# Moving the later adaLN sums of a hybrid decoder layer in VectorE's order, with weights loaded two pieces ahead

## The chip, the core and the metric

One core of a Trainium2 chip runs the kernel. Its engines are called as the profile calls them: PE (TensorE, matrix products; PEld is its loading of weights), DVE (VectorE), ACT (ScalarE), POOL (GpSimd) and SP (SyncE, which issues most transfers). The metric is the device time of one execution in microseconds (us), the median over runs.

## What is computed

One decoder layer on 256 tokens of width 2048, in float32, with matrix products accurate to about float32 (each operand is split into a rounded high part and a low rest). Cut to what matters here:

```python
c_act = silu(c)                                    # one vector of 2048
mod = c_act @ w_mod + b_mod                        # w_mod is 2048 x 12288
shift1, scale1, gate1, shift2, scale2, gate2 = split(mod, 6)     # vectors 0 to 5
u = rms(h, norm1_w) * (1 + scale1) + shift1
proj = u @ w_in                                    # q, k, v of two mixers, z, gates
o_a = stick_breaking(qa, ka, va)                   # 16 heads
o_b = gated_delta_rule(qb, kb, vb, g, beta)        # 16 heads, after a causal convolution
merged = sigmoid(gate_a) * (o_a @ p_a) + sigmoid(gate_b) * (o_b @ p_b)
h = h + gate1 * (merged @ w_out)
u = rms(h, norm2_w) * (1 + scale2) + shift2
h = h + gate2 * ((silu(u @ w_gate) * (u @ w_up)) @ w_down)
```

There are six adaLN vectors of 2048 columns; numbers 0 and 1 are needed at once, 2 (`gate1`) for the output projection, 3 and 4 (`shift2`, `scale2`) for the feed-forward part, 5 (`gate2`) at its end.

## The kernel before

**Jobs and steps.** All large products run through `run_jobs`. A job is one 512-column block of a weight, a step is 256 rows of it (512 KB). For a step, SP loads `raw` (four buffers; the load of step n+4 is issued behind the low split of step n, L277 to L300), ACT rounds it to `wh` (L284), DVE subtracts to get `wl` (a line of `tt`, L119), three steps ahead of use, and PE multiplies activations with both (`mm`, L116; written `acc`). There are two calls of `run_jobs`: the first has the q, k, v blocks of both mixers, three z blocks and the first gate; the second has `p_a`, the last z block, the second gate, `p_b`, `w_out` and the whole feed-forward part.

**Work beside the products.** After each quarter of a step, `beat` advances two queues of Python generators: `convs` (the convolution, on DVE) and `chains`: first four delta-rule chains (`gdn_chain`, one per group of four heads, tiles named `gw`), then four attention chains (`sb_chain`, tiles `sbw`, `SPh`). A delta-rule chain is a long line of small DVE steps between two 128x512 stream transposes, and then of small products (`pb_X`, `pb_Q`, ...) on PE. PE's queue is in order: a `pb_X` whose operand is late holds up every `acc` product behind it.

**The later adaLN sums** are the `background` queue. Every `bg_every` ticks (a tick is half a step) `pump_bg` advances one generator by one yield. `mod_steps` (L176) loads one piece of `w_mod`, 128 rows by 1024 columns, 512 KB, called `wm`, through SP, one piece ahead in two buffers, and adds it, multiplied by one element of `c` per partition, to the sums `macc` (128 x 2048) on DVE (through `stt`, L122; 1024 columns at a time). A vector takes 32 pieces. The 128 partitions are then added up: for vectors 3 and 4 by transposes on PE and accumulating copies on ACT (`mod_cols`, L201), for the gate vectors 2 and 5 by a product with ones (`mod_bcast`, L213). In the first call (`bg_every=3`, from tick 200 on) vectors 3 and 4 are queued, in the second (`bg_every=6`) vector 2, and from the start of the feed-forward part vector 5; in the wide gate jobs of that part a pump comes every 2 ticks, in its up jobs none.

**What sets the order.** The Python program only writes the work down. The framework's planner then lists each engine's instructions by its own estimate of when operands are there, so an instruction can stand far ahead of where it was written. `tc.keep_in_program_order(ins)` ties one instruction behind the instruction written before it on the same engine.

Of the kernel before, what the change touches and what calls it, by code (L numbers as in the profile page):

```python
# [9 lines left out]
F32 = mybir.dt.float32  # L10
F32R = mybir.dt.float32r
AF = mybir.ActivationFunctionType
ALU = mybir.AluOpType
# [3 lines left out]
P = 128  # L17
D = 2048
T = 256
NB = T // P  # L20
KT = D // P
# [6 lines left out]
MW = 1024  # L28
# [4 lines left out]
PUMP_GA = 1.3  # L33
NZ = 3
BGF = 200
BGE = 3
H2 = 5
RG = 2
SMA = 8
# [56 lines left out]
def body(tc, cst, x, c, w_mod, b_mod, norm1_w, w_in, q_norm_w, k_norm_w, conv_w, a_log, dt_bias,  # L96
         o_norm_w, p_a, p_b, w_out, norm2_w, w_gate, w_up, w_down, out, dbg=None):
    nc = tc.nc
    ctx = ExitStack()
    x, w_mod, b_mod, w_in, p_a, p_b, w_out, w_gate, w_up, w_down, out, conv_w = (  # L100
        t[0] for t in (x, w_mod, b_mod, w_in, p_a, p_b, w_out, w_gate, w_up, w_down, out, conv_w))
# [7 lines left out]
    def bank(name, tag="ms"):  # L109
        return ps.tile([P, 512], F32, tag=tag, name=name)  # L110
# [26 lines left out]
    def tr(o, i):  # L137
        nc.tensor.transpose(o, i, ident)
# [19 lines left out]
    n1c, n2c, cc = cols[:, 0:16], cols[:, 16:32], cols[:, 32:48]  # L158
    onc = cols[:, 50:51]
    bsh1, bsc1, bsh2, bsc2 = (cols[:, 64 + 16 * i:80 + 16 * i] for i in range(4))  # L160
# [10 lines left out]
        nc.gpsimd.tensor_tensor(out=o, in0=i, in1=half[:, 0:o.shape[-1]], op=ALU.pow)  # L171


    def mod_steps(i, acc, pool, width, bufs, row, cc=cc):
        v0 = i * D
        if row:  # L176
            nc.gpsimd.memset(acc, 0.0)
            nc.sync.dma_start(out=acc[0:1], in_=b_mod[v0:v0 + D].rearrange("(o d) -> o d", o=1))
        parts = [(k, j) for k in range(KT) for j in range(0, D, width)]
        tiles = {}  # L180

        def load(n):
            k, j = parts[n]
# [15 lines left out]
    def mod_cols(acc, o, bias):  # L199
        for j in range(4):  # L200
            b = bank("pb_mod")  # L201
            for i in range(4):
                tr(b[:, i * P:(i + 1) * P], acc[:, (4 * j + i) * P:(4 * j + i + 1) * P])
            for i in range(4):
                k = 4 * j + i

                act(b[:, i * P:(i + 1) * P], b[:, i * P:(i + 1) * P], AF.Copy, accum_out=o[:, k:k + 1])
            yield
        tt(o, o, bias, ALU.add)
        yield  # L210

    def mod_bcast(acc, o, pool):
        for j in range(4):  # L213
            sl = slice(j * 512, (j + 1) * 512)
            hi = pool.tile([P, 512], F32R, tag="c2", name="bch", bufs=4)
            lo = pool.tile([P, 512], F32R, tag="c2", name="bcl", bufs=4)
            nc.scalar.copy(out=hi, in_=acc[:, sl])
            tt(lo, acc[:, sl], f32(hi), ALU.subtract)
# [5 lines left out]
            yield  # L224


    chains = deque()
# [9 lines left out]
    tph = {}  # L237
# [18 lines left out]
            pump(1000)  # L256

    background = deque()

    def pump_bg(n=1):  # L260
# [109 lines left out]
    mcols = cp.tile([P, 4, KT], F32, name="mcols")  # L370
# [567 lines left out]
    jobs = []  # L938
# [161 lines left out]
    def mod_col_task(i, slot):  # L1100
        acc = tph["tp"].tile([P, D], F32, tag="macc", name="macc", bufs=1)
        yield from mod_steps(i, acc, tph["tp"], MW, 2, False)
        yield from mod_cols(acc, mcols[:, slot], {3: bsh2, 4: bsc2}[i])

    background.append(mod_col_task(3, 3))
    background.append(mod_col_task(4, 2))
    st = {}


    def z_done(n):  # L1110
# [109 lines left out]


    def gate_task(i, key, cc):
        acc = tq.tile([P, D], F32, tag="macc2", name="macc2", bufs=1)
        yield from mod_steps(i, acc, tq, 1024, 2, True, cc)
        st[key] = tq.tile([P, D], F32, tag="gbc", name=key, bufs=1)
        yield from mod_bcast(acc, st[key], tq)
# [22 lines left out]


    def ffn_begin():
        r2 = cp.tile([P, 2], F32, name="r2")
        for b in range(NB):
            act(ss[:, 3, 4 * b:4 * b + 4], ss[:, 2, 4 * b:4 * b + 4], AF.Identity, scale=1.0 / D, bias=eps4, accum_out=r2[:, b:b + 1])
        rstd2 = cp.tile([P, 2], F32, name="rstd2")
        rsqrt(rstd2, r2)
        b2 = cp.tile([P, KT], F32, tag="gate", name="b2", bufs=1)
        nc.gpsimd.tensor_copy(out=b2, in_=mcols[:, 3])
        nc.vector.tensor_scalar(out=mcols[:, 2], in0=mcols[:, 2], scalar1=1.0, scalar2=None, op0=ALU.add)
        tt(mcols[:, 2], mcols[:, 2], n2c, ALU.mult)  # L1260
# [132 lines left out]
```

## Time and profile before

| | before |
|---|---|
| runs, us | 2080.69, 2071.72, 2079.27 (median 2079.27) |
| profiled execution, us | 2075.31, its span 2073.4 |
| PE busy | 1987.6 us (96%) |
| DVE busy | 1380.0 us (67%) |
| ACT busy | 1061.7 us (51%) |
| transfers | 449.72 MB, mean 217 GB/s |
| chain that ended last, by engine | PE 83%, DMA 7%, DVE 5% |

The span is the time from the first to the last instruction; the execution's own time has 1.9 us around it. Busy times are averages over stages with different limits, so what counts is read stage by stage: where PE, the busiest engine, stands still, and what it waited for there. A row of a wait says who waited, on which line, for whom, how long in total and how often. A granted clock (PEclk) of 1.00 is 2.4 GHz; the only other level is 1.2 GHz, so 0.91 over 20 us is a part of that stretch at half speed.

### The profile page before, as it was taken

How to read it: one execution, taken by the hardware profiler on the slowest of the kernel's cores; microseconds unless marked ns; L12 is line 12 of the kernel's file. 1: busy time of each engine (PE TensorE's matmuls, PEld its weight loads, DVE VectorE, ACT ScalarE, POOL GpSimd, SP SyncE). 2: the span in 40 equal slices, each digit the busy share in tenths (PEclk: the TensorE clock that was granted, in tenths of full speed). 3: DMA queues.
4: the chain of work that ended last, by engine and by line, in shares of the span. 5: the costliest groups of instructions: out<-in, count | busy, mean ns of one | idle time of the engine just before them, and what ended most of it. 6: DMA issues, size and time to landing. Idle time of an engine off the chain costs nothing.

```text
span 2073.4 us, 29277 instructions
## 1 busy us (share of the span) xinstructions
PE 1987.6 (96%) x11097; PEld 1719.3 (83%) x11097; DVE 1380.0 (67%) x1846; ACT 1061.7 (51%) x1766; POOL 114.0 (5%) x139
## 2 busy tenths in 40 slices
PE   1999999999999999999999999999999999999998
PEld 1899999987888788887888888788888888888887
DVE  4987989987557876667654555787656555555554
ACT  3346676675666568443454444554455334445432
POOL 4311010110100000000000000000000000000000
PEclk9899999999999999999999999999999999999999
DMA  8996663665557874888766566598755556655563
GB/s 302 386 329 201 194 193 119 208 193 164 167 177 246 291 242 144 255 303 297 237 187 195 184 220 194 178 304 301 227 180 188 195 191 188 190 185 186 190 211 134
DMA packets 208551, 449.72 MB, mean 217 GB/s; under 512 B 16101, under 2 KB 16536, under 8 KB 207896
## 3 DMA queue, kind: packets, MB, share of 16 engines
q1 hardware_dynamic: 198906, 413.25, 62.1%
q0 software_dynamic: 9504, 34.61, 4.5%
q8 instruction: 87, 1.43, 0.3%
q14 instruction: 54, 0.44, 0.1%
HBM read 445.70 MB, written 2.10 MB: 216 GB/s over the span
## 4 chain that ended last, share of the span: by engine, by line
PE 83%; DMA 7%; DVE 5%; issue 2%; ACT 2%; POOL 0%; SPq 0%; DVEq 0%; ACTq 0%; POOLq 0%
PE acc L116 76%; DMA wm<-in_w_mod 4%; DVE wl L119 2%; DMA smod<-in_w_mod 1%; DMA crow<-in_conv_w 1%; PE pb_mod L116 1%; PE pb_Q L116 1%; DVE macc L122 1%; DMA raw<-in_w_in 0%; PE pb_oa L116 0%; PE pb_z L116 0%; ACT wh L284 0%; PE pb_X L116 0%; PE pb_af L116 0%; DVE gw L119 0%
## 5 line engine op out<-in xcount | busy, mean ns | idle before, releaser
L119 DVE TENSOR_TENSOR wl<-raw,wh 128x1024 fp32r<-128x1024 f32 x648 | 789.0, 1221 | 482.2 <-ACT wh L284 479.6
L284 ACT CAST wh<-raw 128x1024 fp32r<-128x1024 f32 x648 | 680.2, 1051 | 768.0 <-PE acc L116 626.4
L116 PE MATMUL acc<-u,wh 128*128 128x512 f32 x1408 | 495.8, 397 | 0.0
L116 PE MATMUL acc<-u,wl 128*128 128x256 f32 x1408 | 395.6, 281 | 2.1 <-DVE wl L119 2.1
L116 PEld LDWEIGHTS acc<-u,wh 128*128 128x128 f32 x1408 | 264.3, 188 | 63.8
L116 PE MATMUL acc<-wh,uh 128*128 128x512 f32 x768 | 307.2, 400 | 0.0
L116 PE MATMUL acc<-wl,uh 128*128 128x512 f32 x768 | 300.6, 391 | 0.0
L116 PE MATMUL acc<-wh,ul 128*128 128x512 f32 x768 | 300.2, 391 | 0.0
L116 PEld LDWEIGHTS acc<-u,wl 128*128 128x128 f32 x1408 | 266.0, 189 | 3.6 <-DVE wl L119 3.3
L116 PE MATMUL acc<-uh,wh 128*128 128x256 f32 x768 | 221.2, 291 | 1.7 <-ACT part L935 1.7
L116 PE MATMUL acc<-uh,wl 128*128 128x256 f32 x768 | 219.4, 287 | 0.0
L116 PE MATMUL acc<-ul,wh 128*128 128x256 f32 x768 | 218.7, 286 | 0.0
L116 PE MATMUL acc<-wh,ff 128*128 128x512 f32 x704 | 216.9, 389 | 0.0
L116 PEld LDWEIGHTS acc<-wl,uh 128*128 128x128 f32 x768 | 144.5, 188 | 30.5
L116 PEld LDWEIGHTS acc<-wh,ul 128*128 128x128 f32 x768 | 144.8, 189 | 27.3
L116 PEld LDWEIGHTS acc<-wh,uh 128*128 128x128 f32 x768 | 144.9, 189 | 26.9
L122 DVE SCALAR_TENSOR_TENSOR macc<-wm,cols,macc 128x1024 f32<-128x1024 f32 x92 | 117.7, 1282 | 59.7 <-DMA wm<-in_w_mod 59.4
L116 PEld LDWEIGHTS acc<-wh,ff 128*128 128x128 f32 x704 | 132.0, 188 | 27.4
L116 PEld LDWEIGHTS acc<-uh,wh 128*128 128x128 f32 x768 | 149.1, 196 | 2.7 <-ACT part L935 1.9
L116 PEld LDWEIGHTS acc<-ul,wh 128*128 128x128 f32 x768 | 148.9, 194 | 0.4
L116 PEld LDWEIGHTS acc<-uh,wl 128*128 128x128 f32 x768 | 148.3, 194 | 0.4
L116 PE MATMUL acc<-wl,ff 128*128 128x512 f32 x352 | 137.0, 389 | 0.0
(289 smaller groups left out, 2268.9 us busy)
## 6 DMA issues: line engine op xcount, KB each, us to landing
raw<-in_w_in SPq DMA_DIRECT2D x286, 512.0 KB, 4.3
wm<-in_w_mod SPq DMA_DIRECT2D x128, 512.0 KB, 5.2
raw<-in_w_gate SPq DMA_DIRECT2D x88, 512.0 KB, 4.3
raw<-in_w_up SPq DMA_DIRECT2D x88, 512.0 KB, 4.4
raw<-in_w_down SPq DMA_DIRECT2D x88, 512.0 KB, 4.2
smod<-in_w_mod POOLq DMA_DIRECT2D x64, 512.0 KB, 11.2
raw<-in_p_a SPq DMA_DIRECT2D x32, 512.0 KB, 5.5
raw<-in_p_b SPq DMA_DIRECT2D x32, 512.0 KB, 3.6
```

The lines of the kernel that those rows point to most:

```text
L116: nc.tensor.matmul(o, lhsT=lhsT, rhs=rhs, start=start, stop=stop, skip_group_check=True)
L119: nc.vector.tensor_tensor(out=o, in0=a, in1=b, op=op)
L122: nc.vector.scalar_tensor_tensor(out=o, in0=a, scalar=s, in1=b, op0=op0, op1=op1, **kw)
L284: nc.scalar.copy(out=wh, in_=raws[n])
```

## The change

Four things are changed together.

1. **Order on DVE.** Every sum of a later adaLN vector is tied behind the DVE instruction written before it (`keep_in_program_order`). It can no longer be listed ahead of its place.
2. **Halves.** A vector is summed in two halves of 1024 columns, all 16 pieces of one half first, in one `macc` of 128 x 1024; the final addition over partitions follows each half (512 columns per yield).
3. **Loads two pieces ahead**, in three buffers (`MRB = 3`), one load to a pump before the first sum.
4. **Where the vectors stand.** Only vector 3 stays in the first call, with a pump every 6 ticks; vectors 2 and 4 are in the second call, with a pump every 3 ticks (`BGD`), and 5 in the feed-forward part as before. `wo_begin` pumps only until vector 2 is done, and `ffn_begin` pumps out the rest.

```diff
-BGE = 3
+BGE = 6
+BGD = 3
+MRB = 3
...
-    def mod_steps(i, acc, pool, width, bufs, row, cc=cc):
+    def mod_parts(i, pool, row, cc, use):
         v0 = i * D
-        parts = [(k, j) for k in range(KT) for j in range(0, D, width)]
+        parts = [(h, k) for h in range(D // MW) for k in range(KT)]
         tiles = {}
...
-            t = pool.tile([P, width], F32, tag="mraw", name=f"wm{i}_{n}", bufs=bufs)
-            nc.sync.dma_start(out=t, in_=w_mod[k * P:(k + 1) * P, v0 + j:v0 + j + width])
+            t = pool.tile([P, MW], F32, tag="mraw", name=f"wm{i}", bufs=MRB)
+            nc.sync.dma_start(out=t, in_=w_mod[k * P:(k + 1) * P, v0 + h * MW:v0 + (h + 1) * MW])
             tiles[n] = t
 
-        load(0)
-        for n, (k, j) in enumerate(parts):
-            if n + 1 < len(parts):
-                load(n + 1)
+        for n in range(MRB - 1):
+            load(n)
+            yield
+        for n, (h, k) in enumerate(parts):
+            if n + MRB - 1 < len(parts):
+                load(n + MRB - 1)
+            if k == 0:
+                acc = pool.tile([P, MW], F32, tag="macc", name="macc", bufs=1)
+                if row:
+                    nc.gpsimd.memset(acc, 0.0)
+                    nc.sync.dma_start(out=acc[0:1], in_=b_mod[v0 + h * MW:v0 + (h + 1) * MW].rearrange("(o d) -> o d", o=1))
+                    yield
             t = tiles.pop(n)
             if k or row:
-                stt(acc[:, j:j + width], t, cc[:, k:k + 1], acc[:, j:j + width], ALU.mult, ALU.add)
+                ins = nc.vector.scalar_tensor_tensor(out=acc, in0=t, scalar=cc[:, k:k + 1], in1=acc, op0=ALU.mult, op1=ALU.add)
             else:
-                nc.vector.tensor_scalar(out=acc[:, j:j + width], in0=t, scalar1=cc[:, 0:1], scalar2=None, op0=ALU.mult)
+                ins = nc.vector.tensor_scalar(out=acc, in0=t, scalar1=cc[:, 0:1], scalar2=None, op0=ALU.mult)
+            tc.keep_in_program_order(ins)
             yield
+            if k == KT - 1:
+                for j in range(MW // 512):
+                    yield from use(h * (MW // 512) + j, acc[:, j * 512:(j + 1) * 512])
...
-    background.append(mod_col_task(3, 3))
-    background.append(mod_col_task(4, 2))
+    background.append(mod_cols(3, mcols[:, 3], bsh2, BgPool(), cc))
...
     background.append(gate_task(2, "g1", cc))
+    background.append(mod_cols(4, mcols[:, 2], bsc2, tq, cc))
...
-        pump_bg(1000)
+        while "g1" not in ready:
+            pump_bg(1)
...
     def ffn_begin():
+        pump_bg(1000)
...
-    run_jobs(jobs, bg_every=6)
+    run_jobs(jobs, bg_every=BGD)
```

**The order it makes.** Three places in the listed order matter below. `macc` is a sum, `wl` a low split, `gw` the third delta-rule chain's tiles, `gq` and `gk` the convolution.

DVE, in the third delta-rule chain, between its two 128x512 stream transposes. Before:

```order
L119 TENSOR_TENSOR gw_3902<-gw_3901 128x112
L122 SCALAR_TENSOR_TENSOR macc<-wm_17_5883,cols,macc 128x1024
L119 TENSOR_TENSOR gw_3901<-gw_3901,gw_3902 128x14x8
L119 TENSOR_TENSOR wl<-raw,wh 128x1024
L119 TENSOR_TENSOR gw_3902<-gw_3901 128x112
L122 SCALAR_TENSOR_TENSOR macc<-wm_18_5929,cols,macc 128x1024
L119 TENSOR_TENSOR gw_3901<-gw_3901,gw_3902 128x16x7
```

After:

```order
L121 TENSOR_TENSOR gw_3901<-gw_3901,gw_3902 128x12x9
L121 TENSOR_TENSOR gw_3902<-gw_3901 128x112
L121 TENSOR_TENSOR gw_3901<-gw_3901,gw_3902 128x14x8
L121 TENSOR_TENSOR gw_3902<-gw_3901 128x112
L121 TENSOR_TENSOR gw_3901<-gw_3901,gw_3902 128x16x7
L121 TENSOR_TENSOR wl<-raw,wh 128x1024
```

The sums have gone from between the chain's steps, and so have some of the splits and convolution steps: from the first stream transpose to the last of the 16 small ones, 9 `wl`, 3 sums and 16 convolution steps stood there before; now there are 6, none and 5. In all, 32 sums stood ahead of the 114th `wl` before; now the first stands behind the 112th `wl`, followed by one about every three `wl` up to the 210th; those of vectors 2 and 4 lie between the 257th and the 371st `wl`, and those of vector 5 between the 391st and the 459th.

PE, at the first small product of the same chain; `acc_4466` and `acc_4467` are the two accumulators of one 512-column block, `wh_4334` the first weight tile of that block. Before:

```order
L116 MATMUL acc_4467<-uh_212,wh_4562 128x256
L116 MATMUL acc_4467<-ul_213,wh_4562 128x256
L116 MATMUL acc_4467<-uh_212,wl_4564 128x256
L116 MATMUL pb_X_4345<-gw1_3902 64x64 x4
L116 MATMUL acc_4467<-uh_212,wh_4562 128x256
```

After:

```order
L118 MATMUL acc_4466<-uh_212,wl_4336 128x256
L118 MATMUL acc_4467<-uh_212,wh_4334 128x256
L118 MATMUL pb_X_4345<-gw1_3902 64x64 x4
L118 MATMUL acc_4467<-ul_213,wh_4334 128x256
L118 MATMUL acc_4467<-uh_212,wl_4336 128x256
```

The chain's first small product now stands 98 `acc` products of 256 columns earlier. In the first and second chain it stands 35 and 9 such products earlier, in the fourth 47 products of 512 columns.

DVE, at the start of the heads of the third attention chain (`sbw<-pb_z` is the first thing DVE does for a head, `SPl` what PE waits for). Before:

```order
L122 SCALAR_TENSOR_TENSOR macc<-wm_16_7406,cols,macc 128x1024
L122 SCALAR_TENSOR_TENSOR macc<-wm_17_7444,cols,macc 128x1024
L119 TENSOR_TENSOR wl<-raw,wh 128x1024 x2
L122 SCALAR_TENSOR_TENSOR macc<-wm_18_7480,cols,macc 128x1024
L119 TENSOR_TENSOR wl<-raw,wh 128x1024
L122 SCALAR_TENSOR_TENSOR macc<-wm_19_7530,cols,macc 128x1024
L119 TENSOR_TENSOR wl<-raw,wh 128x1024
L122 SCALAR_TENSOR_TENSOR macc<-wm_20_7570,cols,macc 128x1024
L122 SCALAR_TENSOR_TENSOR sbw<-pb_z,a 128x384 x2
L119 TENSOR_TENSOR sbw<-sbw,cs 128x2x128
L119 TENSOR_TENSOR wl<-raw,wh 128x1024
L119 TENSOR_TENSOR SPl<-sbw,SPh 128x384
```

After:

```order
L202 SCALAR_TENSOR_TENSOR macc<-wm_6872,cols,macc 128x1024
L202 SCALAR_TENSOR_TENSOR macc<-wm_6947,cols,macc 128x1024
L121 TENSOR_TENSOR wl<-raw,wh 128x1024 x6
L202 SCALAR_TENSOR_TENSOR macc<-wm_7010,cols,macc 128x1024
L124 SCALAR_TENSOR_TENSOR sbw<-pb_z,a 128x384 x2
L121 TENSOR_TENSOR sbw<-sbw,cs 128x2x128
L121 TENSOR_TENSOR wl<-raw,wh 128x1024
L121 TENSOR_TENSOR SPl<-sbw,SPh 128x384
```

Five sums stood within four splits there; now one stands behind six splits.

## Rows read from the trace of the kernel before

**Rows 1.** Busy time by stage: us, engines' busy (instructions), PEclk, DMA share, GB/s.

```profile
170.00:330.00 160.00, 155.13 (x1307) 151.91 (x1306) 143.75 (x315) 108.97 (x250) 14.81 (x15) 0.99 0.61 189
330.00:450.00 120.00, 113.66 (x970) 108.39 (x969) 107.58 (x234) 79.89 (x220) 16.62 (x19) 0.97 0.55 172
450.00:510.00 60.00, 56.15 (x338) 45.68 (x337) 52.30 (x121) 43.01 (x94) 4.90 (x4) 1.00 0.64 192
510.00:640.00 130.00, 129.92 (x632) 108.78 (x631) 73.16 (x100) 85.92 (x211) 9.69 (x9) 1.00 0.53 160
...
700.00:730.00 30.00, 25.44 (x110) 20.73 (x109) 23.88 (x28) 14.44 (x23) 0.00 (x0) 0.94 0.86 291
...
850.00:930.00 80.00, 80.00 (x354) 66.26 (x353) 53.20 (x44) 34.90 (x36) 0.00 (x0) 1.00 0.88 296
930.00:990.00 60.00, 55.84 (x238) 43.80 (x236) 42.98 (x38) 22.04 (x23) 0.00 (x0) 1.00 0.88 299
...
1050.00:1276.00 226.00, 226.00 (x1016) 186.66 (x1015) 122.43 (x120) 102.10 (x115) 1.81 (x1) 1.00 0.61 197
1335.00:1435.00 100.00, 100.00 (x576) 87.84 (x575) 79.26 (x83) 47.21 (x61) 0.00 (x0) 1.00 0.89 300
1435.00:1460.00 25.00, 22.86 (x128) 19.31 (x127) 20.18 (x21) 10.25 (x15) 0.00 (x0) 1.00 0.89 312
```

**Rows 2.** Groups in 850:930: busy us, mean ns, idle before them and its end.

```profile
L116 PE MATMUL acc<-wh,uh 128*128 128x512 f32 x118 | 45.9, 389 | 0.0
L119 DVE TENSOR_TENSOR wl<-raw,wh 128x1024 fp32r<-128x1024 f32 x27 | 32.5, 1220 | 7.8 <-ACT wh L284 7.6
L122 DVE SCALAR_TENSOR_TENSOR macc<-wm,cols,macc 128x1024 f32<-128x1024 f32 x17 | 21.8, 1285 | 17.7 <-DMA wm<-in_w_mod 17.4
```

**Rows 3.** Groups in 930:990.

```profile
L116 PE MATMUL acc<-wh,oah 128*128 128x512 f32 x77 | 30.1, 390 | 0.0
L122 DVE SCALAR_TENSOR_TENSOR macc<-wm,cols,macc 128x1024 f32<-128x1024 f32 x14 | 18.0, 1284 | 18.7 <-DMA wm<-in_w_mod 18.7
```

**Rows 4.** Instructions on `wm`, whole span: time from issue to landing.

```profile
DMA to landing us min/median/max: 3.4/5.2/6.8
```

**Rows 5.** Timeline of DVE, 696:717: start, us, instruction, [idle before, its end].

```profile
708.62 1.28 DVE L122 SCALAR_TENSOR_TENSOR macc<-wm,cols,macc 128x1024 f32<-128x1024 f32 x1 [4.43 <-DMA wm<-in_w_mod]
```

**Rows 6.** Timeline of PE, 709:716.

```profile
714.10 0.45 PE L116 MATMUL pb_af<-SPh,rmask 128*128 128x384 f32 x1 [3.95 <-ACT SPh L1039]
715.16 0.69 PE L116 MATMUL pb_af<-SPl,rmask 128*128 128x384 f32 x1 [0.61 <-DVE SPl L119]
```

**Rows 7.** Busy time by stage, shorter stretches, columns as in rows 1.

```profile
78.00:104.00 26.00, 23.79 (x164) 23.08 (x165) 22.41 (x27) 8.36 (x12) 9.57 (x14) 0.80 1.03 386
...
710.00:730.00 20.00, 15.44 (x65) 12.64 (x65) 19.01 (x24) 9.66 (x15) 0.00 (x0) 0.91 0.88 294
```

**Rows 8.** Timeline of PE at the chains' first small products, four windows.

```profile
250.13 0.45 PE L116 MATMUL pb_X<-gw 128*64 128x64 f32 x8 [2.44 <-issue]
...
335.13 0.45 PE L116 MATMUL pb_X<-gw 128*64 128x64 f32 x8 [1.87 <-ACT gw L125]
...
416.42 0.45 PE L116 MATMUL pb_X<-gw 128*64 128x64 f32 x8 [2.12 <-issue]
...
495.40 0.45 PE L116 MATMUL pb_X<-gw 128*64 128x64 f32 x8 [1.42 <-issue]
```

**Rows 9.** Instructions on `macc` in 170:510: forms, and the waits before them.

```profile
L122 DVE SCALAR_TENSOR_TENSOR macc<-wm,cols,macc x30: 1274/1279/1287, 180.7 to 477.8; 128x1024 f32<-128x1024 f32 x30
...
  DMA wm<-in_w_mod: 9.6, 7
```

**Rows 10.** Groups of DVE in 380:420, by form.

```profile
L119 DVE TENSOR_TENSOR wl<-raw,wh 128x1024 fp32r<-128x1024 f32 x11 | 13.3, 1213 | 0.3 <-ACT wh L284 0.3
L122 DVE SCALAR_TENSOR_TENSOR gk<-acc,cw,gk 128x254 f32<-128x254 f32 x4 | 1.9, 474 | 0.0
```

**Rows 11.** Instructions on `wm` in 1335:1460: the waits before them.

```profile
  DMA wm<-in_w_mod: 21.3, 16
```

More of the change, by code (lines that the diff above doesn't have):

```diff
@@ L171, in rsqrt @@
         nc.gpsimd.tensor_tensor(out=o, in0=i, in1=half[:, 0:o.shape[-1]], op=ALU.pow)
-    def mod_steps(i, acc, pool, width, bufs, row, cc=cc):
+    def mod_parts(i, pool, row, cc, use):
         v0 = i * D
-        if row:
-            nc.gpsimd.memset(acc, 0.0)
-            nc.sync.dma_start(out=acc[0:1], in_=b_mod[v0:v0 + D].rearrange("(o d) -> o d", o=1))
-        parts = [(k, j) for k in range(KT) for j in range(0, D, width)]
+        parts = [(h, k) for h in range(D // MW) for k in range(KT)]
@@ L180, in mod_steps @@
         tiles = {}
         def load(n):
-            k, j = parts[n]
-            t = pool.tile([P, width], F32, tag="mraw", name=f"wm{i}_{n}", bufs=bufs)
-            nc.sync.dma_start(out=t, in_=w_mod[k * P:(k + 1) * P, v0 + j:v0 + j + width])
+            h, k = parts[n]
+            t = pool.tile([P, MW], F32, tag="mraw", name=f"wm{i}", bufs=MRB)
+            nc.sync.dma_start(out=t, in_=w_mod[k * P:(k + 1) * P, v0 + h * MW:v0 + (h + 1) * MW])
             tiles[n] = t
-        load(0)
-        for n, (k, j) in enumerate(parts):
-            if n + 1 < len(parts):
-                load(n + 1)
+        for n in range(MRB - 1):
+            load(n)
+            yield
@@ L195, in mod_steps @@
             else:
-                nc.vector.tensor_scalar(out=acc[:, j:j + width], in0=t, scalar1=cc[:, 0:1], scalar2=None, op0=ALU.mult)
+                ins = nc.vector.tensor_scalar(out=acc, in0=t, scalar1=cc[:, 0:1], scalar2=None, op0=ALU.mult)
+            tc.keep_in_program_order(ins)
             yield
-    def mod_cols(acc, o, bias):
-        for j in range(4):
-            b = bank("pb_mod")
[L202 to L207, printed above, removed]
+            if k == KT - 1:
+                for j in range(MW // 512):
+                    yield from use(h * (MW // 512) + j, acc[:, j * 512:(j + 1) * 512])
@@ L208, in mod_cols, with use, mod_bcast @@
+    def mod_cols(i, o, bias, pool, cc):
+        def use(q, acc):
+            b = bank("pb_mod")
+            for n in range(4):
+                tr(b[:, n * P:(n + 1) * P], acc[:, n * P:(n + 1) * P])
+            for n in range(4):
+                k = 4 * q + n
+                act(b[:, n * P:(n + 1) * P], b[:, n * P:(n + 1) * P], AF.Copy, accum_out=o[:, k:k + 1])
             yield
+        yield from mod_parts(i, pool, False, cc, use)
         tt(o, o, bias, ALU.add)
         yield
-    def mod_bcast(acc, o, pool):
-        for j in range(4):
-            sl = slice(j * 512, (j + 1) * 512)
+    def mod_bcast(i, o, pool, cc):
+        def use(q, acc):
+            sl = slice(q * 512, (q + 1) * 512)
@@ L215, in mod_bcast @@
             hi = pool.tile([P, 512], F32R, tag="c2", name="bch", bufs=4)
             lo = pool.tile([P, 512], F32R, tag="c2", name="bcl", bufs=4)
-            nc.scalar.copy(out=hi, in_=acc[:, sl])
-            tt(lo, acc[:, sl], f32(hi), ALU.subtract)
+            nc.scalar.copy(out=hi, in_=acc)
+            tt(lo, acc, f32(hi), ALU.subtract)
             yield
@@ L224, in mod_bcast @@
             yield
+        yield from mod_parts(i, pool, True, cc, use)
     chains = deque()
@@ L258, in body, with tile @@
     background = deque()
+    class BgPool:
+        def tile(self, *a, **kw):
+            return tph["tp"].tile(*a, **kw)
     def pump_bg(n=1):
@@ L1097, in body @@
             jobs.append(Job(w_in, (OFF_SBQ, OFF_SBK, OFF_SBV)[i] + g * 512, uact, done, pump=PUMP_S if g else PUMP_GL))
[L1100 to L1103, printed above, removed]
-    background.append(mod_col_task(3, 3))
-    background.append(mod_col_task(4, 2))
+    background.append(mod_cols(3, mcols[:, 3], bsh2, BgPool(), cc))
     st = {}
+    ready = set()
     def z_done(n):
@@ L1222, in gate_task @@
     def gate_task(i, key, cc):
-        acc = tq.tile([P, D], F32, tag="macc2", name="macc2", bufs=1)
-        yield from mod_steps(i, acc, tq, 1024, 2, True, cc)
         st[key] = tq.tile([P, D], F32, tag="gbc", name=key, bufs=1)
-        yield from mod_bcast(acc, st[key], tq)
+        yield from mod_bcast(i, st[key], tq, cc)
+        ready.add(key)
     background.append(gate_task(2, "g1", cc))
+    background.append(mod_cols(4, mcols[:, 2], bsc2, tq, cc))
     def wo_begin():
```

## The prediction, made before the changed kernel ran

> **What bounds the kernel now.** I read the stages first: busy time in stretches that I cut where PE stops being full [rows 1]. PE is the bound nearly everywhere. From 510 to 640 it works 129.92 of 130 us, from 1050 to 1276 all of 226, and in the feed-forward part from 1335 to 1435 all of 100. So time can only be won where PE stands still, and rows 1 show four such places behind the opening: 170 to 510, 700 to 730, 930 to 990 and 1435 to 1460. (The opening, before 170, and the start of the feed-forward part are not touched.) Then I read, place by place, who ended the wait.
>
> In 930 to 990 a product costs PE 80 us / 354 = 0.226 us when it is not held up (118 rows of each of three kinds in 850 to 930 [rows 1, 2]), so a step of 12 products is 2.71 us. From 850 to 930 DVE does 17 sums and 27 splits and waits 17.4 us for `wm` [rows 2]; PE still has splits in stock and is full. From 930 DVE is busy 42.98 us and waits 18.7 us for `wm` [rows 1, 3]: 61.7 us in a stretch of 60. DVE has no time left, although three tenths of its time is waiting, and PE loses 4.16 us by its idle time. At 708.6 one sum waited 4.43 us for its piece [rows 5]; behind it in DVE's queue stood another split, another sum and the head's own work, and PE waited 3.95 and 0.61 us for that [rows 6].
>
> **Part by part.** The sum is made against the profiled execution, 2075.31 us; the median of the runs is 3.96 us above it.
>
> *No work disappears.* The 128 sums and their loads stay: 1.28 us each on DVE [rows 9], 512 KB each. Two further clearings of `macc` on POOL and two further loads of `b_mod` rows are small and lie off PE's path. POOL and SP get them early, in their places in the queue; if the clearing came late, SP would hold up the `raw` loads behind it, and the cover there is the four `raw` buffers, 4 x 2.71 = 10.8 us. One wait is new: with a single `macc` the first sum of the second half has to wait until the first half has been read out, and `wl` splits stand behind it on DVE. In the order nine splits (the 156th to the 165th, some 24 us) lie between the two for vector 3, so I price it at nothing.
>
> *Term 1, 930 to 990: minus 6.* With a pump every 3 ticks, three steps (8.13 us) hold two sums and three splits: 2 x 1.28 + 3 x 1.22 = 6.2 us [rows 2], which fits, without the waits. Two pieces ahead means 2 x 3 ticks, 8.1 us, against a landing of 5.2 us in the median and 6.8 at most [rows 4]; so the waits go. The loss here is 4.16 us by idle time. By count it is larger: PE has about 3 x 77 = 231 products in 60 us [rows 3], 52 us' worth, so 8 us are missing; short waits hide inside the modelled ends of the products. I take 6, the middle.
>
> *Term 2, 700 to 730: minus 6.* PE idles 30 - 25.44 = 4.56 us [rows 1], and right behind it the granted clock is 0.91 over 20 us [rows 7]: part of it ran at 1.2 GHz, which costs another 0.09 x 20 = 1.8 us. Together 6.4. In the changed order one sum, its piece fetched two pumps of 6 ticks (16 us) ahead, stands behind six splits where five stood within four. I take 6.
>
> *Term 3, 1435 to 1460: minus 2.5, plus 1.* Idle 2.14 us; by count 128 rows against 576 / 4 = 144, 16 x 0.174 = 2.8 us [rows 1]. Its cause is the same, 21.3 us of waits for `wm` in 1335 to 1460 [rows 11]. Now vector 5 gets eight pumps in each gate job and none in an up job, so in a gate job (128 products x 0.174 = 22.2 us) 8 + 8 pieces, 8.39 MB, are wanted: 378 GB/s. Rows 1 show 312 at most in this part; at that rate a gate job falls 4.7 us behind, which 8 us of splits in stock cover, and the up job catches up. But the opening shows 386 GB/s [rows 7]. I take 1 us for five such jobs, between 0 and 5. The Trainium skill, "DMA: Bandwidth & Descriptors", section "Bandwidth", has a lower limit for one core, about 358 GB/s from HBM. By that rule each gate job would end 1.2 us late and, if nothing were caught up, the sum would have 5 x 1.2 = 6 us in place of 1. The 386 GB/s of rows 7 are above it, so the row decides.
>
> *Term 4, 170 to 510: minus 3.* PE idles 4.87 + 6.34 + 3.85 = 15.1 us here [rows 1], and the delta-rule chains on DVE cause it: `pb_X` waits 2.44, 1.87, 2.12 and 1.42 us in the four chains [rows 8]. All 32 sums of vector 3 leave this stretch, with 9.6 us of waits for `wm` [rows 9]. It is tempting to count the 15 us as won. The order speaks against it: the planner has already spent the relief. In the third chain DVE has 3 sums, 3 splits and 11 convolution steps fewer between the two stream transposes, 3 x 1.28 + 3 x 1.21 + 11 x 0.47 = 12.6 us [rows 9, 10], but PE comes to `pb_X` 98 products of 0.12 us (113.66 us / 970 in 330 to 450 [rows 1]), 11.8 us, earlier. In the first chain the products come 35 x 0.12 = 4.2 us earlier against three sums and the wait before them. So the stalls stay, about as long. What the planner had not reckoned with is the waiting for `wm`; a third of its 9.6 us I count as won, since only some of these waits fell while DVE was full. Ends: minus 9.6, if all of it was on the path; plus 8, if each of the four stalls grows by 2 us because the relief falls short.
>
> *Term 5, the new places of the sums: plus 1.* 510 to 640, where DVE is busy 73 of 130 us, gets a sum every 8 us; 1050 to 1276, where it is busy 122 of 226, gets one every 4 us, some 60 us more, about 80% [rows 1]. The cover is the stock of three splits, 8.1 us. The nearest row is 850 to 930, the same rate of sums with waits on top and PE full (80.00 of 80), so 0; the other end is the rival below. `ffn_begin` finds nothing left: 44 pumps for vector 2 and 39 for vector 4 need 249 ticks, and the jobs ahead have 272.
>
> Sum: -6 - 6 - 2.5 + 1 - 3 + 1 = -15.5 us. The profiled execution would be 2059.8; from the median, 2079.27 - 15.5 = **2063.8**, forecast 2064.
>
> **The rivals.**
> *The chains take it back.* Term 4 is +8 in place of -3, where the small products on PE have been moved further than DVE's relief reaches; this decides in the third and fourth chain, moved by 11.8 and 10.6 us. For it: relief and move are within a microsecond of each other in the third chain, and the planner's estimates were already short by 1.4 to 2.4 us in all four [rows 8]. Against: the waits for `wm` are gone. Time: 2064 + 11 = 2075, no change.
> *The transfers are the limit (slower).* If not the single piece ahead but the transfers themselves made DVE wait in 930 to 990 (0.88 of their time busy, 299 GB/s [rows 1]), a third buffer helps nothing, and the loss of that stretch, 6 us in 60, spreads over all 114 steps between the 257th and 371st split, 309 us: 31 us, 25 more than now. With terms 2 and 4 unchanged and nothing from term 3 that is 2079.3 + 25 - 9 = 2095. It decides when landing takes over 8.1 us. Against it: 6.8 us at most [rows 4], at that same load.
> *The chains run free.* Terms 1 and 4 at their ends, -8 and -9.6: 2055. It needs every wait for `wm` to have been on the path.
>
> **How the numbers follow.** Forecast 0.55, chains take it back 0.25, transfers 0.08, chains free 0.12. The range reaches from 2050 (the lower rival, and 5 us for where in their spread of 9 us the runs fall) to 2078 (the "no change" rival and 3 us); it leaves out the slower rival and the tails. About 0.5%, 10.4 us, is what a measurement can tell here: faster means under 2068.9. That is four fifths of the forecast, the lower rival and a tenth of "no change": 0.44 + 0.12 + 0.02 = 0.58. Slower 0.08. The rest, 0.34, is the same.
>
> **What would show it.** Right: no row of DVE waiting for `wm` above 2 us in all behind 500; PE full from 640 to 730 and from 930 to 1276; no granted clock under 1.00 near 710; `pb_X` still waiting 1 to 3 us in each chain. Wrong: waits for `wm` or `raw` in 957 to 1276 or in the gate jobs; a `pb_X` wait of 4 us or more; more than 1 us of PE idle from 510 to 640, where sums are new. If all waits for `wm` are gone and the time is the same, the chains took it.

## The result and the profile after

| | before | after |
|---|---|---|
| median, us (runs) | 2078.87 (4) | 2055.39 (4: 2056.12, 2054.83, 2052.0, 2055.94) |
| ratio, 95% interval | | 0.9886, 0.9869 to 0.9904 |
| profiled execution, span | 2075.31, 2073.4 | 2056.12, 2054.1 |

The change is faster by 1.1%. The medians lie 23.5 us apart, the two profiled executions 19.2; the profile of before happens to lie 3.6 us under its median. Below, the terms are compared with the 19.3 us between the two spans.

Busy time by stage after the change, columns and stretches as in [rows 1], without 850 to 930:

```profile
170.00:330.00 160.00, 155.26 (x1322) 152.00 (x1323) 135.14 (x318) 113.14 (x259) 13.89 (x15) 1.00 0.48 148
330.00:450.00 120.00, 116.03 (x971) 110.09 (x969) 97.56 (x227) 84.75 (x235) 15.23 (x20) 0.96 0.40 119
450.00:510.00 60.00, 56.97 (x353) 47.59 (x352) 43.84 (x103) 37.16 (x91) 3.65 (x3) 0.97 0.48 138
510.00:640.00 130.00, 130.00 (x609) 108.52 (x608) 90.46 (x112) 82.73 (x166) 8.39 (x8) 1.00 0.71 228
700.00:730.00 30.00, 30.00 (x140) 25.16 (x140) 22.58 (x31) 17.16 (x25) 0.00 (x0) 1.00 0.68 217
...
930.00:990.00 60.00, 60.00 (x267) 49.69 (x266) 47.02 (x43) 23.19 (x22) 0.00 (x0) 1.00 0.89 302
1050.00:1276.00 226.00, 225.97 (x1020) 186.58 (x1020) 167.30 (x160) 104.45 (x142) 0.95 (x1) 1.00 0.87 297
1335.00:1435.00 100.00, 100.00 (x569) 86.97 (x568) 69.29 (x77) 51.58 (x69) 0.95 (x1) 1.00 0.78 256
1435.00:1460.00 25.00, 25.00 (x147) 22.06 (x146) 17.65 (x20) 11.86 (x15) 0.00 (x0) 1.00 0.67 205
```

700 to 730, 930 to 990 and 1435 to 1460, where PE stood still before, are full, and where the sums went (510 to 640, 1050 to 1276) PE stays full although DVE is busier. Of these stretches only 170 to 510 still has gaps to speak of: 4.74 + 3.97 + 3.03 = 11.7 us by idle time, 15.1 before.

A stretch of fixed times cuts the work at another point in each kernel. So I also take the start of five products that both kernels have, in PE's timeline: the first 512-column product of the input projection, of `p_a`, of `w_out`, the first transpose of the feed-forward part, and the first product of `w_down`. Before:

```profile
442.19 0.40 PE L116 MATMUL acc<-wh,uh 128*128 128x512 f32 x1
931.62 0.39 PE L116 MATMUL acc<-wh,oah 128*128 128x512 f32 x1
1229.38 0.39 PE L116 MATMUL acc<-wh,mh 128*128 128x512 f32 x1
1322.71 0.92 PE L138 MATMUL pb_u<-cs,hn 128*128 128x128 f32 x3 [4.61 <-DVE hn L1264]
1602.08 0.64 PE L116 MATMUL acc<-wh,ff 128*128 128x512 f32 x2
```

After:

```profile
437.95 0.40 PE L118 MATMUL acc<-wh,uh 128*128 128x512 f32 x1
919.93 0.39 PE L118 MATMUL acc<-wh,oah 128*128 128x512 f32 x1
1212.63 0.39 PE L118 MATMUL acc<-wh,mh 128*128 128x512 f32 x1
1306.42 0.87 PE L140 MATMUL pb_u<-cs,hn 128*128 128x128 f32 x3 [4.70 <-DVE hn L1281]
1582.92 0.63 PE L118 MATMUL acc<-wh,ff 128*128 128x512 f32 x2
```

| from one to the next | before | after | difference |
|---|---|---|---|
| start to `uh` (chains one to three) | 442.19 | 437.95 | -4.2 |
| to `oah` (fourth chain, attention) | 489.43 | 481.98 | -7.5 |
| to `mh` (`p_a`, gate, `p_b`) | 297.76 | 292.70 | -5.1 |
| to `hn` (`w_out`) | 93.33 | 93.79 | +0.5 |
| to `ff` (gate and up jobs) | 279.37 | 276.50 | -2.9 |
| to the end of the span | 471.32 | 471.18 | -0.1 |

In these two executions all of the time comes from where sums stood before. From `hn` to `ff` an execution can differ by some 3 us by itself: runs eight, nine, ten and twelve below, which have the change's code from there on, took 273.4 to 274.2 us for it and not 276.50. On DVE in 930 to 990, what [rows 3] were:

```profile
L121 DVE TENSOR_TENSOR wl<-raw,wh 128x1024 fp32r<-128x1024 f32 x23 | 28.2, 1225 | 14.5 <-ACT wh L304 14.5
L202 DVE SCALAR_TENSOR_TENSOR macc<-wm,cols,macc 128x1024 f32<-128x1024 f32 x14 | 17.9, 1279 | 0.0
```

As many sums, 14, in the same 60 us, with no wait where 18.7 us were. The waiting has moved to the splits, which now wait for ACT's `wh`: DVE has room again. In the whole span (instructions on `wm`, answering to [rows 4]):

```profile
  DMA wm<-in_w_mod: 9.7, 9
DMA to landing us min/median/max: 3.6/5.6/8.1
```

The pieces land no sooner than before (5.2 us in the median then). What is left of the waits lies in the gate jobs. The four first small products of the chains, what [rows 8] were (PE's timeline, four windows):

```profile
243.93 0.45 PE L118 MATMUL pb_X<-gw 128*64 128x64 f32 x8 [1.42 <-issue]
...
329.71 0.70 PE L118 MATMUL pb_X<-gw 128*64 128x64 f32 x8 [2.88 <-ACT gw L127]
...
399.62 0.69 PE L118 MATMUL pb_X<-gw 128*64 128x64 f32 x8 [3.94 <-issue]
...
479.37 0.62 PE L118 MATMUL pb_X<-gw 128*64 128x64 f32 x8 [3.00 <-issue]
```

The last three wait longer than before (1.87, 2.12, 1.42).

### The profile page after: what moved, and what is told of

It is laid out like the page before. It is cut to its first block, busy times and chain, and to the rows that moved or that the text cites. A ratio compares the mean times of both kernels' runs of the same rounds, so it can differ in the third digit from the quotient of the medians.

```text
span 2054.1 us, 29271 instructions
## 1 busy us (share of the span) xinstructions
PE 1983.1 (97%) x11097; PEld 1720.7 (84%) x11097; DVE 1386.4 (67%) x1846; ACT 1064.9 (52%) x1766; POOL 108.9 (5%) x141
## 4 chain that ended last, share of the span: by engine, by line
PE 93%; DMA 3%; DVE 2%; issue 1%; ACT 1%; POOL 0%; SPq 0%; DVEq 0%; ACTq 0%; POOLq 0%
PE acc L118 85%; DMA smod<-in_w_mod 1%; DMA crow<-in_conv_w 1%; PE pb_mod L118 1%; PE pb_Q L118 1%; DMA raw<-in_w_in 0%; PE pb_oa L118 0%; PE pb_z L118 0%; PE pb_X L118 0%; DVE wl L121 0%; PE pb_af L118 0%; DVE accb L124 0%; PE pb_o L118 0%; PE pb_u L118 0%; PE pb_tr L140 0%
## 5 line engine op out<-in xcount | busy, mean ns | idle before, releaser
L304 ACT CAST wh<-raw 128x1024 fp32r<-128x1024 f32 x648 | 680.2, 1050 | 776.7 <-PE acc L118 694.9
```

The lines of the kernel that those rows point to most:

```text
L304: nc.scalar.copy(out=wh, in_=raws[n])
```

## Experiments

The prediction gave the gain to the second piece of lead. The first four runs set that ("waits") against the order alone ("order"). All were timed in one set with the kernel before, 2077.67 us.

**One: without the tie.**

```diff
-            tc.keep_in_program_order(ins)
```

> The changed kernel without the tie that keeps a sum in its place on DVE; halves, two pieces ahead and the places of the vectors stay. In the listed order 16 of the 32 sums of vector 3 then stand among the first 100 splits again, inside the delta-rule chains. Theory 'waits' (the gain is the waits for wm that fell while DVE was full, and two pieces ahead remove them): DVE's waits for wm stay under 20 us in all (81 before, 10 after), 640 to 990 stays full, and the time is within 5 us of the changed kernel, 2052 to 2060. Rival 'order' (the gain is that sums no longer stand in bunches ahead of what PE waits for): the stalls before the small products at 300 to 480 and the one near 710 come back, 2065 or more.

Measured: 2068.81 us, ratio 0.9955 (0.9938 to 0.9972). More than half of the gain is gone, 8.9 us are left, and the waits for `wm` are back, 82.4 us, with the third buffer in place. DVE, groups of 930 to 990:

```profile
L202 DVE SCALAR_TENSOR_TENSOR macc<-wm,cols,macc 128x1024 f32<-128x1024 f32 x13 | 16.7, 1284 | 16.1 <-DMA wm<-in_w_mod 16.1
```

**Two: tied, one piece ahead.**

```diff
-MRB = 3
+MRB = 2
```

> The changed kernel with one piece ahead in two buffers, all else kept, the tie too. Theory 'waits': in the second call a piece is then asked for 3 ticks, some 4.1 us, ahead against a landing of 5.6 us in the median, so most of the 64 sums of vectors 2 and 4 wait 1 to 2 us, DVE's waits for wm are 60 us or more, DVE is overfull in 930 to 990, and the time is 2063 to 2080. Rival 'order': the stock of splits covers these waits, and the time is within 4 us of the changed kernel, 2051 to 2060.

Measured: 2054.48 us, ratio 0.9879 (0.9859 to 0.9899), no different from the change. The same group:

```profile
L202 DVE SCALAR_TENSOR_TENSOR macc<-wm,cols,macc 128x1024 f32<-128x1024 f32 x15 | 19.2, 1280 | 0.0
```

Fifteen sums, one piece ahead, and no wait (the 33.3 us that this kernel has in all lie behind 990, where PE is full or nearly so). So the second piece of lead is worth nothing here, and the tie is what removes the waits. My figure of 4.1 us of lead against a landing of 5.6 was wrong: in this trace DVE comes to the sums of 930 to 990 6.9 us (median) after their loads were issued, and those loads land in 5.7. That fits a DVE that works on a stock of splits and so runs behind the loads by more than one pump.

**Three: the kernel before with the tie alone.**

```diff
-                stt(acc[:, j:j + width], t, cc[:, k:k + 1], acc[:, j:j + width], ALU.mult, ALU.add)
+                ins = nc.vector.scalar_tensor_tensor(out=acc[:, j:j + width], in0=t, scalar=cc[:, k:k + 1],
+                                                     in1=acc[:, j:j + width], op0=ALU.mult, op1=ALU.add)
...
+            tc.keep_in_program_order(ins)
```

> The kernel before with the tie alone: one piece ahead, whole vectors, vectors 3 and 4 in the first call every 3 ticks. All sums leave the first 100 splits; 64 then stand between the 100th and the 210th. Theory 'waits': the waits for wm stay at 60 us or more, now spread over places where DVE has some room; 930 to 990 gets only one sum per three splits, so part of its loss goes, and the time is 2066 to 2080. Rival 'order': the tie alone gives most of the gain, 2052 to 2063.

Measured: 2056.4 us, ratio 0.989 (0.9872 to 0.9907). One edit of four gives the whole gain; on top of it halves, lead and the vectors' places add nothing that can be measured. Without it they are not worth nothing: run one, which has these three alone, is 8.9 us under the kernel before, with PE at 206.00 of 206 in 1335 to 1541 and 28.16 of 30 in 700 to 730 (25.44 before). Which of the three does that was not tried. Vectors 3 and 4 are both in the first call here, 17 sums stand in 640 to 730, and PE is full there (90.00 of 90).

**Four: the kernel before with two pieces ahead for the gate vectors, untied.**

```diff
-        load(0)
+        for n in range(bufs - 1):
+            load(n)
...
-            if n + 1 < len(parts):
-                load(n + 1)
+            if n + bufs - 1 < len(parts):
+                load(n + bufs - 1)
...
-        yield from mod_steps(i, acc, tq, 1024, 2, True, cc)
+        yield from mod_steps(i, acc, tq, 1024, 3, True, cc)
```

> The kernel before with vectors 2 and 5 loaded two pieces ahead in three buffers, no tie, all else as before (vectors 3 and 4 still one piece ahead). Theory 'waits': the 18.7 us of waits for wm in 930 to 990 and the 21.3 us in 1335 to 1460 go, and with them the idle time of PE in those two places: 6 and 2.5 us, the time is 2066 to 2073, and the stall of 4 us near 710 stays. Rival 'order': bunches of sums still stand ahead of the splits, DVE stays full, and the time is within 4 us of the kernel before, 2074 or more.

Measured: 2075.37 us, ratio 0.9987 (0.9974 to 1.0001). In 930 to 990:

```profile
L122 DVE SCALAR_TENSOR_TENSOR macc<-wm,cols,macc 128x1024 f32<-128x1024 f32 x14 | 18.0, 1285 | 19.8 <-DMA wm<-in_w_mod 19.6
```

Again 14 sums and 19.6 us of waits. In the old places a third buffer without the tie gives nothing (run four), in the new places a buffer less under the tie takes nothing (run two), and the tie gives in both (run three, and the change against run one). Both of my theories had a half of it. Waiting is what cost, since 14 sums stand in 930 to 990 in the kernel before and in the change, with 18.7 us of waits and with none; but the waits come from the place. Vector 2's sums are written one per 3 splits, and untied they are listed one per 1.4 (all 32 between the 224th and the 268th split). Tied, the same sums stand from the 254th to the 347th split.

What this does to the lead can be read by setting the issue of a load in SP's timeline against the moment when DVE came to its sum, which is the sum's start less the idle time before it. One piece of run four, and one of run three:

```profile
952.58 0.46 SPq L185 DMA_DIRECT2D wm<-in_w_mod  x1
957.62 1.28 DVE L122 SCALAR_TENSOR_TENSOR macc<-wm,cols,macc 128x1024 f32<-128x1024 f32 x1 [1.74 <-DMA wm<-in_w_mod]
...
940.75 0.34 SPq L185 DMA_DIRECT2D wm<-in_w_mod  x1
955.76 1.28 DVE L194 SCALAR_TENSOR_TENSOR macc<-wm,cols,macc 128x1024 f32<-128x1024 f32 x1
```

In run four DVE came 957.62 - 1.74 - 952.58 = 3.3 us behind the load, in run three 15.0. Over the sums of 930 to 990 (medians, each with the landing of the loads there):

| | DVE behind the load, us | landing, us |
|---|---|---|
| kernel before | 4.7 | 5.4 |
| run four (third buffer, untied) | 5.1 | 5.8 |
| run one (third buffer, new places, untied) | 5.6 | 6.5 |
| run two (tied, two buffers) | 6.9 | 5.7 |
| change (tied, three buffers) | 11.6 | 5.5 |
| run three (old places, tied, two buffers) | 15.0 | 5.2 |

DVE waits where the first number lies under the second, and the third buffer alone moved the first by only 0.4 us. What SP waited for in run four, 930 to 990, shows why:

```profile
SPq L280 <- DVE wl L119: 43.3, 19, 4.9
```

That is the only row: SP never waits there for a buffer of `wm`. For 43.3 of 60 us it stands at a `raw` load, until DVE has done a split, and the `wm` loads stand behind these in SP's queue (the one at 952.58 right behind the `raw` load at 952.16). Why the planner lists the sums so early was not tried. The Trainium skill, "PSUM — Partial Sum Buffer", section "Engine vs sequencer instructions", says that the queues of ScalarE, VectorE and GpSimdE are strict FIFO. The traces agree: in [rows 5, 6] PE's wait at 714 ended with work that stood behind the waiting sum.

**Five and six: each half of the tie alone**, in the kernel before. On the gate vectors 2 and 5, against the kernel of three:

```diff
-            tc.keep_in_program_order(ins)
+            if row:
+                tc.keep_in_program_order(ins)
```

On vectors 3 and 4 the same with `if not row:`.

> The kernel before with the tie on the sums of the gate vectors 2 and 5 alone, those that stand in 850 to 990 and 1335 to 1460. Vectors 3 and 4 keep their old places, and the chains their old order. Theory 'the untied listing makes the waits, and they cost where DVE is full': 930 to 990 and 1435 to 1460 become full, terms 1 and 3 of the prediction, 6 to 8 and 2 to 3 us: 8 to 11 us under the kernel before, 2064 to 2069. Rival 'it is the chains' stretch that gave': under 4 us of gain, 2072 or more.

> The kernel before with the tie on the sums of vectors 3 and 4 alone. The four delta-rule chains get the listed order of the changed kernel, and 700 to 730 one sum per 1.5 splits; the gate vectors stay untied, and vector 2 stands between the 224th and the 268th split. Theory as for the other half: the stall near 710 and the clock behind it go (6 us), the chains' stretch changes by no more than 3 us either way, 930 to 990 keeps most of its loss: 2066 to 2072. Rival 'it is the chains' stretch that gave': 10 us or more of gain, 2066 or less, and PE's idle time in 170 to 510 with what the clock takes there falls by 6 us or more.

Measured, beside 2077.37 us: 2064.61 us, ratio 0.994 (0.9927 to 0.9952), and 2066.55 us, ratio 0.9954 (0.9942 to 0.9967). The product of the two, 0.9894, is the ratio of the whole tie, 0.989, within the intervals. Windows of the first, tied gates:

```profile
510.00:730.00 220.00, 216.05 (x1026) 180.30 (x1025) 149.68 (x193) 136.96 (x309) 15.38 (x14) 0.99 0.68 217
850.00:990.00 140.00, 140.00 (x620) 115.91 (x619) 74.71 (x63) 59.10 (x61) 0.00 (x0) 1.00 0.72 222
1335.00:1541.00 206.00, 206.00 (x1185) 181.21 (x1184) 146.99 (x160) 103.55 (x137) 0.00 (x0) 1.00 0.81 262
```

And of the second, tied vectors 3 and 4:

```profile
510.00:730.00 220.00, 220.00 (x1038) 183.98 (x1037) 172.59 (x213) 141.12 (x302) 16.37 (x14) 1.00 0.82 268
850.00:990.00 140.00, 135.96 (x587) 108.80 (x586) 98.10 (x84) 55.93 (x57) 0.00 (x0) 1.00 0.89 297
1335.00:1541.00 206.00, 204.94 (x1158) 177.42 (x1157) 145.04 (x158) 101.29 (x135) 0.00 (x0) 1.00 0.80 258
```

Both came as the first theory had it; the idle time in 170 to 510 fell by 3.1 us in the second, at the edge of the first theory's 3 and not by the rival's 6. Each half heals its own places and leaves the others. Read down 510 to 730: with 23 us more of DVE work than the first, the second has PE full and the first 4 us short.

**Seven: nearly no sums.**

```diff
             h, k = parts[n]
+            if k:
+                return
```

(and the sums of these pieces with them: the kernel leaves out 15 of every 16.)

> The changed kernel without 15 of every 16 later sums and without their loads (vectors 2 to 5 are then wrong: only the first 128 rows of w_mod count). This is the floor: what the sums still cost. PE's listed order is that of the changed kernel. Theory 'order' (tied sums stand behind a stock of splits and cost PE nothing): within 5 us of the changed kernel, 2048 to 2058, with the same four waits before the small products, 1.4, 2.9, 3.9 and 3.0 us. Rival 'DVE is still short' (short waits hidden in the modelled ends of the products, or the transfers beside them, still take time): 2035 to 2046.

Measured: 2052.82 us, ratio 0.989 (0.9875 to 0.9905), not to be told from the change, with the four waits at `pb_X` at 1.44, 2.92, 3.95 and 3.00 us. The 120 sums left out, 120 x 1.28 = 154 us of DVE and 63 MB of transfers, cost nothing, and what waits in the chains has nothing to do with them. With PE's order as it is, no better place for the sums is worth looking for.

**Eight: a pump every 2 ticks.**

```diff
-BGD = 3
+BGD = 2
```

> The changed kernel with a pump every 2 ticks in place of 3 in the second call (BGD = 2), tied, two pieces ahead. From the 255th to the 332nd split there is then a sum per 1.2 splits: 2.5 us of DVE per 2.71 us, and 512 KB of wm beside 512 KB of raw per 2.71 us, 387 GB/s wanted. Theory 'order' with DVE's and the transfers' limits taken from the earlier profiles (DVE 43 of 60 us and 0 waits are harmless; at most 312 GB/s were seen here): the transfers fall short, 1.05 MB take 3.3 us or more, so waits for wm or raw come back in 930 to 1150 and some 60 steps lose up to 0.6 us each: 2060 to 2095. Rival 'the stock is enough': 2051 to 2058, and over 350 GB/s in that stretch.

Measured: 2056.64 us, ratio 0.9909 (0.9894 to 0.9924).

```profile
930.00:1150.00 220.00, 219.11 (x986) 181.09 (x985) 181.64 (x165) 100.32 (x121) 0.95 (x1) 1.00 0.94 330
```

The transfers give 330 GB/s over 220 us with PE at 219.11, and DVE is 83% busy. The rival is nearer, though its 350 GB/s was not reached: PE came through that stretch without needing it. My expectation of a lack was wrong, since it took the highest rate seen in [rows 1], 312, for a limit.

**Nine to twelve: the chains.** What is left in 170 to 510 is PE's wait at `pb_X`. The edit is one number, `BD`, the beat at which a chain's first small product is written (19 before), here for the first two runs:

```diff
-BD = 19
+BD = 22
```

```diff
-BD = 19
+BD = 25
```

> The changed kernel with the first small product of a delta-rule chain written three beats later (BD = 22 for 19). In the listed order it moves by 46 products of 256 columns in the third chain, 5.5 us, and by 2 of 512 in the fourth; in the first two chains it does not move. Theory 'listed too early' (PE waits at pb_X because the planner's estimate for the chain is 1.4 to 4 us short): the third wait, 3.94 us, goes and the others stay, and with the clock behind it the time is 4 to 6 us shorter, 2048 to 2053. Rival 'the chain itself is late': the wait moves to a later product of the chain or to its end, 2054 to 2060.

> The changed kernel with that product written six beats later (BD = 25). It moves by 47 products of 256 columns in the third chain, 5.6 us, and by 12 of 512 columns in the fourth, 2.7 us. Theory 'listed too early': the third wait goes and the fourth falls from 3.0 to under 1 us, 6 to 9 us shorter in all, 2046 to 2051. Rival 'the chain itself is late': 2054 to 2062.

Measured, beside 2075.36 us: 2051.17 us, ratio 0.9883 (0.9866 to 0.9899), and 2048.7 us, ratio 0.9868 (0.9854 to 0.9883). The times lie in the ranges of "listed too early", but the kernel before was faster in this set too (2075.36 against 2078.87), and by ratio BD = 22 is no different from the change (0.9886). The waits don't fit. With BD = 22 the fourth grew from 3.00 to 3.99 us, and the third is still there:

```profile
403.66 0.45 PE L118 MATMUL pb_X<-gw 128*64 128x64 f32 x8 [3.20 <-issue]
```

With BD = 25, the third and the fourth:

```profile
403.05 0.45 PE L118 MATMUL pb_X<-gw 128*64 128x64 f32 x8 [2.65 <-issue]
...
478.49 0.45 PE L118 MATMUL pb_X<-gw 128*64 128x64 f32 x8 [3.03 <-ACT gw L127]
```

Listed 46 products, 5.5 us, later, the third product starts 4.0 us later (399.62 before) and waits only 0.7 us less. DVE's timeline shows why. In the changed kernel one split stands between the chain's large transpose and the 16 small ones:

```profile
394.64 1.12 DVE L685 STREAM_TRANSPOSE gw<-gw 128x512 f32<-128x512 f32 x1
395.68 1.19 DVE L121 TENSOR_TENSOR wl<-raw,wh 128x1024 fp32r<-128x1024 f32 x1
396.79 4.05 DVE L711 STREAM_TRANSPOSE gw<-gw 32x64 f32<-32x64 f32 x16
```

With BD = 22 two convolution steps have joined it, and the large transpose itself, with other work put ahead of it, starts 4.0 us later:

```profile
398.64 1.13 DVE L685 STREAM_TRANSPOSE gw<-gw 128x512 f32<-128x512 f32 x1
399.68 0.84 DVE L124 SCALAR_TENSOR_TENSOR gk<-acc,cw,gk 128x253 f32<-128x253 f32 x2
400.43 1.22 DVE L121 TENSOR_TENSOR wl<-raw,wh 128x1024 fp32r<-128x1024 f32 x1
401.56 3.99 DVE L711 STREAM_TRANSPOSE gw<-gw 32x64 f32<-32x64 f32 x16
```

So this relief is spent too, by the order on DVE. In both kernels eight small ACT steps follow the large transpose, and the product comes as they end. ACT's timeline in the changed kernel:

```profile
395.85 3.67 ACT L127 ACTIVATE gw<-gw,cs 32x128 f32<-32x128 f32 x8 [0.81 <-DVE gw L685]
```

395.85 + 3.67 = 399.52, and `pb_X` starts at 399.62. What BD = 25 has over the change in the two profiled executions comes from the clock more than from the waits: idle time in 170 to 510 falls only from 11.7 to 10.9 us, but the granted clock behind the third and fourth wait is higher. The changed kernel behind its third and fourth wait:

```profile
400.00:410.00 10.00, 10.00 (x90) 8.95 (x86) 8.06 (x25) 8.13 (x25) 0.00 (x0) 0.78 0.18 55
480.00:490.00 10.00, 9.97 (x81) 7.84 (x81) 7.02 (x19) 6.37 (x21) 0.00 (x0) 0.85 0.37 107
```

With BD = 25:

```profile
400.00:410.00 10.00, 6.88 (x71) 6.22 (x70) 9.38 (x30) 9.54 (x26) 0.00 (x0) 1.00 0.25 77
480.00:490.00 10.00, 10.00 (x79) 8.08 (x79) 7.97 (x17) 6.65 (x19) 0.00 (x0) 1.00 0.52 159
```

0.22 x 10 + 0.15 x 10 = 3.7 us, with 0.8 us of idle time 4.5 of the 7.7 us between the two spans; 2.3 more lie from `hn` to `ff`, which BD does not touch.

The last two, BD = 25 with the tie alone (the kernel of three), and BD = 30:

> The kernel before with the tie on all sums and the chains' first small products six beats later (BD = 25): two edits, no halves, one piece ahead, vectors where they were. Theory 'the tie is what counts': as the changed kernel with BD = 25, 2044 to 2052. Rival 'the second piece of lead and the places are needed when PE has less idle time': 2053 to 2058.

> The changed kernel with BD = 30. In the listed order the first small product stays where BD = 25 has it in three chains (2, 1 and 0 products of 256 columns off) and moves by 26 further products of 512 columns, 6 us, in the fourth. Theory 'a chain that is written later is also listed later on DVE' (with BD = 22 the third chain's product moved by 5.5 us and its wait only from 3.9 to 3.2): the waits stay at 1.4, 2.9, 2.7 and 2 to 3.5 us, and the time is within 3 us of BD = 25, 2046 to 2052. Rival 'listed too early': the fourth wait goes, 2043 to 2046.

Measured, beside 2077.37 us: 2052.7 us, ratio 0.989 (0.9874 to 0.9907), and 2052.89 us, ratio 0.9885 (0.9872 to 0.9899). The first is on the border of what either theory gave (2052 and 2053) and is not to be told from three, so the two edits together are not shown to be worth more than one. Its third wait is 2.61 us with a clock of 1.00 over 400 to 410, as in the changed kernel with BD = 25, but its clock over 480 to 490 is 0.66: that better clock does not come with BD = 25 as such. BD = 30 gives back what 25 won: the fourth wait is 2.41 us, but the third is 4.27 and the clock of 330 to 450 back at 0.97. Its time lies above both ranges, and by its waits neither theory held. The best version run is the changed kernel with BD = 25: its four runs, 2043.93 to 2049.87, lie under all four of the change, which was timed in another set; the two intervals against the kernel before overlap by a little (0.9883 and 0.9869), and no run compares the two directly.

## Why the prediction was right, and where it was not

**The time.** Forecast 2064 by a sum of -15.5 us, measured 2055.4; on the footing on which the sum was made, profile against profile, -19.3. The direction and the places were right, and in this pair of executions every term came within 1.5 us, on the small side. The reason given for one of the two largest was wrong, and that its size came out all the same is luck of the bundle: the tie, which is part of the same change, did what the prediction put down to the third buffer.

- *Term 1 and term 5* (-6 + 1): -5.1 from `p_a` to `w_out`. Right in size. The step that failed is "Two pieces ahead means 2 x 3 ticks, 8.1 us, against a landing of 5.2 us in the median and 6.8 at most; so the waits go." In 930 to 990 run two has one piece and no wait, run four two pieces and all of them, with DVE only 5.1 us behind the loads. What goes is the early listing, the part of the change that the prediction described for the chains and left out here. The count of 8 us missing was too high as well: it takes 231 of the 238 products of [rows 1], and 238 x 0.226 = 54 us leave 6. Term 5 itself, 0 to 1 us, held: PE is full in 510 to 640 and has lost 0.03 us in 1050 to 1276.
- *Term 2* (-6): -7.5 from the first 512-column product to `p_a`. The granted clock is 1.00 over 700 to 730. The fourth chain lies in this stretch too and gave nothing: the first `pb_z` product starts 108.46 us behind the first `uh` product before and 108.48 after. Run five, which leaves vectors 3 and 4 untied, keeps the loss.
- *Term 3* (-2.5 + 1): -2.9. Too small by 1.4 us, and by up to 4.5 with the 273.4 us of other executions, since no gate job was late. The rate that I wanted there, 378 GB/s, was not asked for on the mean of gate and up jobs: 256 over 1335 to 1435, at most 337 in a stretch of 11 us, with PE at 100.00 of 100. The limit of 358 GB/s, which I weighed there, is by the Trainium skill, "HBM Reference", section "Specifications (TRN2)", the share of a core whose neighbour streams too; a core alone gets well above it. The 386 GB/s of [rows 7] agree.
- *Term 4* (-3): -4.2. "So the stalls stay, about as long" held for `pb_X`, and run seven, whose chains are listed as in the change, has the same four waits with nearly no sums. Two things were not foreseen, and they cancel in part. The waits at `pb_X` grew from 7.9 us [rows 8] to 11.2 in all, and three waits of the chains at other products, which I had not read in PE's timeline of before, are gone:

```profile
306.16 0.63 PE L138 MATMUL pb_at<-cs,gw 128*128 128x128 f32 x4 [1.74 <-DVE gw L119]
...
385.36 0.63 PE L138 MATMUL pb_at<-cs,gw 128*128 128x128 f32 x4 [2.35 <-DVE gw L119]
...
454.49 0.50 PE L116 MATMUL pb_d<-Gl,rmask 128*128 128x512 f32 x1 [1.62 <-DVE Gl L119]
```

- *Transfers as the limit*: refuted; run eight asks for more and PE loses 0.89 us in 220. *Chains take it back*: in part, as the three grown waits and 0.97 in 450 to 510 show, but the other waits paid for it. *Chains run free* gave 2055, the time that was measured, by the wrong terms: -8 and -9.6 where -5.1 and -4.2 came.
- *The signs.* PE full and clock 1.00 near 710: seen. `pb_X` waits 1.4, 2.9, 3.9 and 3.0 us: the third is above the 1 to 3 us of "right", and just under the 4 us of "wrong". "No row of DVE waiting for `wm` above 2 us in all behind 500" was not: 9.7 us are left, 9.2 of them from 1335 to 1541, gate and up jobs, which I had listed as a sign against. They cost nothing, since PE is full there. A wait is a sign only where its engine has no stock.

## What to carry to other kernels

When an engine with an in-order queue waits for transfers, look first whether the waiting instruction stands earlier than it was written: pinning it to its place gave 1.1% here, and a deeper buffer without the pin nothing. Read the lead off the trace, from the issue of the load to the moment when the engine comes to its use, and compare it with the landing; a count of buffers does not tell it. A wait costs only where the engine has no time left in that stretch; read busy plus waiting time against the length of the stretch. Where a planner fills gaps by its own estimates, relief given to a chain is spent again, so price it from the new order and not from the work taken away.

## What the runs showed of the hardware

- The granted clock does not follow the length of the wait ahead of it: behind a wait of 3.00 us it was 0.85 (480 to 490 after the change), behind one of 3.03 us 1.00 (BD = 25, same stretch), behind one of 2.88 us 0.66 (run eleven, same stretch), and before the change 0.91 over the 10 us that hold a wait of 2.12. What else decides was not tried. That the clock can make more of a difference than the waits, 3.7 us between two executions whose idle time in the chains differs by 0.8, I had not expected.
- One core drew 330 GB/s over 220 us with its transfer engines 0.94 busy, and landing took 5.9 us in the median in that run against 5.6 in the change.
